# Order and buffers in a Strassen-form feed-forward layer: a product moved, a fifth weight buffer, and the first difference of a weight tile made first

## The chip, the cores and the metric

The kernel runs on one core of one Trainium2 chip. The metric is the device time of one execution in microseconds (us). Kernel before: 956.69 us, the median of three runs (956.43 to 957.4).

## The reference

One layer of a hybrid decoder over 1,024 tokens and 16 learned meta tokens, width 1,024, all in float32:

```python
u = rmsnorm(h, g_pre_mix[l])
z = u @ w_in[l]
q, k, v, xr, yr = jnp.split(z, split_at, axis=-1)
attn = sliding_window_attention_with_sinks(...)      # window 128, 8 heads of 64
hr = rg_lru(causal_depthwise_conv(xr, ...), ...)     # linear recurrence over the tokens
rec = (jax.nn.gelu(yr.astype(jnp.float32)) * hr).astype(h.dtype)
mix = jnp.concatenate([attn.astype(h.dtype), rec], axis=-1) @ w_out[l]
h = h + rmsnorm(mix, g_post_mix[l])
u = rmsnorm(h, g_pre_ffn[l])
f = jnp.square(jax.nn.relu(u @ w_ff1[l])) @ w_ff2[l]
h = h + rmsnorm(f, g_post_ffn[l])
```

The feed-forward part is 1,024 × 1,024 × 4,096 and back; its two matrix products take most of the time, and the change is there.

## The kernel before

**Numbers.** Every float32 operand of a product is taken apart into a high and a low part in the type fp32r (`split`, L96 and L99): ScalarE casts the tile (high), then VectorE subtracts the cast from the tile (low). A product is then three matmuls (`mm3`, L125 to L127): high × high, high × low, low × high. `product` makes four of these, for four chunks of 128 rows: twelve matmuls with 512 columns.

**Strassen form.** The first product `u @ w_ff1` is done by a Strassen–Winograd scheme over 2 × 2 blocks: seven products of blocks where the plain way has eight, for sums and differences of blocks of weights and of activations. The weights of w_ff1 go through in 16 pairs of chunks (p = 0 to 15), each 128 columns of the left and of the right half. For each pair the products add up into four blocks ("11", "12", "21", "22"), which are later activated (relu, square) and go into w_ff2. The second product has the same form, written as a table of seven steps for each of eight quarters (`PLAN`, `steps`): 56 steps, each with a weight tile from one or two loads. Where there are two, they are combined on VectorE, or added on the way by an accumulating DMA of GpSimd.

**First loop of w_ff1.** `prep_a(p)` makes what pair p needs. It loads two 512 KB tiles by SyncE's queue (`w1_load`, L989): r0, in a buffer named "raw" (two of these), which holds the blocks a11 and a21, and r1 ("a" or "d") with a12 and a22. Four combines (L992, VectorE, 128 × 512 each) follow: a22 + a21, a21 − a11, a3 = that sum − a11, and a12 − a3. Two splits: r0 into a pair of "ws" buffers (128 × 1024; high on ScalarE, low on VectorE), and a3 into one "e" buffer that holds its high and low part. r1, which now has the changed a12 and a22, is stored to `s_dram` by GpSimd's queue (L1037), for the second loop.

The loop over p then issues, for each pair: product with e (a3), a ScalarE copy of the accumulator to block "12" (L1177), product `p1(p+2)` of a11 (which needs ws of that pair), product with the ws columns of a21, and a copy to block "21" (L1181). So an iteration on TensorE is three products. For the first four pairs p1 and p2 ("early" products, with weights loaded ahead: `a11_early`, `a12_early`) are done before the loop. p2 adds its product to block "11" on VectorE (L1106).

Six pieces of other work, `t_rest`, are spread over the iterations p = 3 to 8: four differences of activations, and two splits whose results go to `t4_dram` for a later stage (L1168).

**What sets the order.** The framework places each engine's instructions by priority and by a model of when operands are ready; each engine then runs its list in order. `behind(name, instruction)` adds an edge of order only: the instruction stands after the named one. In w_ff2, `prep_2` puts a combine behind the low part of two steps before (L1264 is the load there, `w_lows`). SyncE and GpSimd issue their DMAs in the order of their lists, and a DMA waits at the head of its list until its buffer is free.

**Buffers.** One table has the number of buffers by name: "raw" 2, "ws" 4, "a" 16, "b" 17, "c" 8, "d" 4, "e" 3. A tile takes the buffers of its name in turn, and waits for the last reader of the tile that had that buffer.

Of the kernel before, what the change touches and what calls it, by code (L numbers as in the profile page):

```python
# [10 lines left out]
F32R = mybir.dt.float32r  # L11
AF = mybir.ActivationFunctionType
ALU = mybir.AluOpType
# [3 lines left out]
P = 128  # L17
# [20 lines left out]
def hybrid_layer(  # L38
# [6 lines left out]
    nc = tc.nc  # L45
# [6 lines left out]
    ps = ctx.enter_context(tc.tile_pool(name="ps", bufs=2, space=PSUM))  # L52
    dpool = ctx.enter_context(tc.tile_pool(name="dpool", bufs=1, space=DRAM))

    bufs = {"raw": 2, "ws": 4, "a": 16, "b": 17, "c": 8, "d": 4, "e": 3}
    uid = [0]

    def slot(tag, shape, dt=F32):
        uid[0] += 1
        return slab.tile(shape, dt, tag=tag, name=f"{tag}{uid[0]}", bufs=bufs[tag])  # L60

    def pair(tag, shape):
        return slot(tag, shape, F32R), slot(tag, shape, F32R)

    def bank(tag, shape=(P, 512)):
        uid[0] += 1
        return ps.tile(list(shape), F32, tag=tag, name=f"ps_{tag}{uid[0]}")

    def f32(ap):
        return ap.bitcast(F32)  # L70
# [23 lines left out]
    def split(hi, lo, src, eng=None):  # L94
        if eng is None:
            nc.scalar.copy(hi, src)  # L96
        else:
            eng.tensor_copy(hi, src)
        low = nc.vector.tensor_tensor(lo, src, f32(hi), op=ALU.subtract).ins  # L99
        mark[0] = low.name  # L100
        return low
# [4 lines left out]
    def behind(name, *inss):  # L106
        for ins in inss:
            tc.add_manual_dep(
                ins, name,
                mybir.DependencyInfo(  # L110
                    mybir.DependencyClass.NoSync, mybir.DependencyReason.DATA
                ),
                reason="order",
            )
# [5 lines left out]
        ).ins  # L120
        return high, low

    def mm3(dst, lhs, rhs, start, stop):
        (lh, ll), (rh, rl) = lhs, rhs
        nc.tensor.matmul(dst, lh, rh, start=start, stop=False, skip_group_check=True)  # L125
        nc.tensor.matmul(dst, lh, rl, start=False, stop=False, skip_group_check=True)  # L126
        last_mm[0] = nc.tensor.matmul(  # L127
            dst, ll, rh, start=False, stop=stop, skip_group_check=True
        ).ins.name

    last_mm = [None]
# [129 lines left out]
    def project(w, pieces, sink):  # L261
        wh, wl = w
        for t0, n in pieces:
            acc = bank("acc")
            for kc in range(KC):
                uh, ul = u[kc]
                mm3(
                    acc[:, :n], (wh[:, kc, :], wl[:, kc, :]),
                    (uh[:, t0 : t0 + n], ul[:, t0 : t0 + n]),
                    kc == 0, kc == KC - 1,  # L270
                )
            sink(acc[:, :n], t0, n)
# [70 lines left out]
    def low_w(w, raw):  # L343
        chained(1, nc.vector.tensor_tensor(w[1], raw, f32(w[0]), op=ALU.subtract).ins)
# [58 lines left out]
    low_w(wv, rv)  # L403
    wq = high_w(rq)
    low_w(wq, rq)
    km = slot("e", [P, 4, 2 * P], F32R)
    nc.gpsimd.memset(f32(km[:, 0:2, 0 : P - NMETA]), 0.0)
    nc.gpsimd.memset(f32(km[:, 2:4, :]), 0.0)
    nsink = const.tile([P, 8], F32, name="nsink")
# [84 lines left out]
    for b in range(4):  # L494
# [3 lines left out]
        if b == 0:  # L498

            acc = [bank("acc"), bank("acc")]  # L500
# [11 lines left out]
            for w, (t0, n), sink, tag in (  # L512
                (wq, (16, 256), sink_q0, "o"), (wx, piece, sink_x0, "acc"),
            ):
                acc = bank(tag)
# [397 lines left out]
    t4_dram = dpool.tile([P, 2, 4, 512], F32, name="t4_dram")  # L913
# [73 lines left out]
    def w1_load(dst, b, p, a0, a1):  # L987
        c0 = 256 * p
        nc.sync.dma_start(dst, w1v[b][:, :, c0 + P * a0 : c0 + P * a1])  # L989

    def combine(dst, x0, x1, op):
        return nc.vector.tensor_tensor(dst, x0, x1, op=op).ins  # L992

    def operand(tiles):
        pairs = []
        for t_ in tiles:
            hi, lo = pair("b", [P, 2, 512])
            split(hi, lo, t_)
            pairs.append((hi, lo))
        return pairs  # L1000

    def product(acc, w, op, first):
        wh, wl = w
        for kc in range(4):
            hh, ll = op[kc // 2]
            mm3(
                acc, (wh[:, kc, :], wl[:, kc, :]), (hh[:, kc % 2, :], ll[:, kc % 2, :]),
                first and kc == 0, kc == 3,
            )

    LO, HI = slice(0, P), slice(P, 2 * P)
# [3 lines left out]
    def prep_a(p, late=None):  # L1015
        r0 = slot("raw", [P, 4, 256])
        w1_load(r0, 0, p, 0, 2)
        r1 = slot("a" if 2 <= p < 6 else "d", [P, 4, 256])
        w1_load(r1, 1, p, 0, 2)
        a11, a21, a12, a22 = r0[:, :, LO], r0[:, :, HI], r1[:, :, LO], r1[:, :, HI]  # L1020
        sums = [
            combine(a22, a21, a22, ALU.add), combine(a21, a11, a21, ALU.subtract)
        ]
        if late:
            behind(late, *sums)
        hi, lo = pair("ws", [P, 4, 256])
        if p in a11_early:
            split(hi[:, :, HI], lo[:, :, HI], a21)
            first = a11_early[p]
        else:  # L1030
            split(hi, lo, r0)
            first = hi[:, :, LO], lo[:, :, LO]
        combine(a11, a22, a11, ALU.subtract)
        hl = slot("e", [P, 2, 4, P], F32R)
        split(hl[:, 0], hl[:, 1], a11)
        combine(a12, a12, a11, ALU.subtract)
        nc.gpsimd.dma_start(s_dram[p], r1)  # L1037
        return first, (hl[:, 0], hl[:, 1]), (hi[:, :, HI], lo[:, :, HI])


    def early(b, p0, hl):
        raw = slot("raw", [P, 2, 4, P])
        for k in range(2):
            w1_load(raw[:, k], b, p0 + k, 0, 1)
        split(*hl, raw)
        return {p0 + k: (hl[0][:, k], hl[1][:, k]) for k in range(2)}

    a11_early, a12_early = {}, {}

    def fetch_b(p):  # L1050
        r1 = slot(("e", "raw")[p % 2], [P, 4, 256])
        nc.sync.dma_start(r1, s_dram[p])
        return r1
# [24 lines left out]
    def block(k, p):  # L1078
        q = p // 2
        if fb[k][q] is None:  # L1080
            fb[k][q] = slot(FTAG[k][q], [P, 2, 512])
        return fb[k][q][:, p % 2, :]
# [15 lines left out]
    def p1(p, w):  # L1098
        ya[p] = bank(("acc", "s")[p // 2 % 2])
        product(ya[p], w, b11, True)  # L1100
        nc.scalar.copy(block("11", p), ya[p])

    def p2(p, w):
        y2 = bank("pt")
        product(y2, w, b21, True)
        nc.vector.tensor_tensor(block("11", p), y2, block("11", p), op=ALU.add)  # L1106

    for t in range(8):
# [12 lines left out]
        if t == 6:  # L1121
            b21 = operand(u2f[0][2:4])
            hl = slot("b", ESH, F32R), slot("e", ESH, F32R)
# [4 lines left out]
    for p in range(2):  # L1128
        p2(p, a12_early[p])
# [10 lines left out]

    t_sums(slice(0, 3 * P))
    wa[0] = prep_a(0)
    u2_tiles(7, xns[7])
    t_sums(slice(3 * P, 4 * P))
# [1 line left out]
    for p in range(2, 4):  # L1146
        p1(p, a11_early[p])
    a12_early.update(early(1, 2, pair("a", ESH)))
    for p in range(2, 4):
        p2(p, a12_early[p])  # L1150
    ot3 = [pair("b", [P, 2, 512]) for _ in range(2)]
    for i in range(2):
        behind(urgent, split(*ot3[i], t3[i]))
# [3 lines left out]
    def t_rest(k):  # L1157
        i = k % 2
        if k < 2:
            behind(mark[0], combine(u2f[1][i], u2f[1][i], u2f[0][i], ALU.subtract))  # L1160
        elif k < 4:
            behind(mark[0], combine(t2[i], u2f[0][2 + i], t2[i], ALU.subtract))
        else:
            hl = pair("a", [P, 2, 512])
            late = mark[0]
            behind(late, split(*hl, t2[i]))
            for n in range(2):
                nc.sync.dma_start(t4_dram[:, n, 2 * i : 2 * i + 2, :], f32(hl[n]))  # L1168

    raw_b, raw_c = {}, {}  # L1170
    for p in range(16):
        if p + 2 < 16:
            wa[p + 2] = prep_a(p + 2, None if p else urgent)
        if p >= 13:
            raw_b[p - 13] = fetch_b(p - 13)
        product(ya[p], wa[p][1], ot2, False)
        nc.scalar.copy(block("12", p), ya[p])  # L1177
        if 4 <= p + 2 < 16:
            p1(p + 2, wa[p + 2][0])
        product(ya[p], wa[p][2], ot3, False)  # L1180
        nc.scalar.copy(block("21", p), ya[p])  # L1181
        if 3 <= p < 9:
            t_rest(p - 3)

        if p == 14:
            ot1 = operand(u2f[1][0:2])
# [81 lines left out]
    def prep_2(n, tag="ws"):  # L1268
        i, q = steps[n]
        fx, wx, _ = PLAN[i]  # L1270
        raws = raw_2.pop(n)
        if len(raws) == 2:
            ins = combine(raws[0], raws[0], raws[1], wx[2])
            if i == 6:
                behind(w_low[0], ins)
            elif i > 2:
                behind(w_lows[n - 2], ins)
        wh, wl = pair(tag, [P, 2, 512])
        w_low[0] = w_lows[n] = split(wh, wl, raws[0]).name
        if len(fx) == 3:  # L1280
            f = slot("b", [P, 2, 512])
            combine(f, fb[fx[0]][q], fb[fx[1]][q], fx[2])
        else:
            f = fb[fx[0]][q]
        fh, fl = pair("b", [P, 2, 512])
        split(fh, fl, f)
        return fh, fl, wh, wl
# [11 lines left out]
    for n, p in enumerate(third):  # L1299
# [8 lines left out]
        if p not in a12_early:  # L1308
            y2 = bank(("acc", "s")[p % 2])
# [195 lines left out]
```

## Time and profile before

| | |
|---|---|
| median of three runs | 956.69 us (956.43 to 957.4) |
| the profiled execution | 955.87 us, of which 954.1 us between the first and the last instruction |
| granted clock of TensorE | 0.999 |
| TensorE busy | 944.0 us, 4728 matmuls |
| VectorE / ScalarE / GpSimd busy | 657.8 / 504.2 / 125.4 us |
| moved by DMA | 130.21 MB, mean 136 GB/s |
| first loop of w_ff1 | about 350 to 475 us |

How to read a line: a timeline row gives start, duration, engine, line of the kernel, operation, output ← inputs, shapes, and in brackets how long the engine was idle before and what it waited for. A row of waits gives who waited for whom, the sum in us, how often, and the longest. A row of stretches gives the stretch, its length, busy time and count for TensorE, its weight loads, VectorE, ScalarE and GpSimd, then the granted clock, the busy share of the DMA engines and GB/s. TensorE's matmuls overlap: one of 512 columns is listed with about 0.39 us, and starts come every 0.23 us. "Issue to landing" of a DMA is told by the trace only for some of them.

### The profile page before, as it was taken

The numbers are of one execution on the slowest core, as the hardware profiler recorded it, in microseconds if no ns is written. First come the engines' busy times: TensorE is split into PE (matmuls) and PEld (weight loads), VectorE is DVE, ScalarE is ACT, GpSimd is POOL, SyncE is SP. The second block draws the span as 40 slices with busy tenths as digits, with TensorE's granted clock in tenths as the row PEclk, the third lists the DMA queues.
The fourth block names the chain that finished last, engine by engine and source line by source line (L and its number), as shares of the span: only waits on it lengthen the run. The fifth ranks groups of instructions, "written<-read, shape, count | busy, mean of one in ns | idle before, by whom it ended". The sixth has DMA issues, their size and how long they took to land.

```text
span 954.1 us, 12400 instructions
## 1 busy us (share of the span) xinstructions
PE 944.0 (99%) x4728; PEld 789.3 (83%) x4728; DVE 657.8 (69%) x845; ACT 504.2 (53%) x854; POOL 125.4 (13%) x184
## 2 busy tenths in 40 slices
PE   9999999999999999999999999999999999999997
PEld 8999999877888877888888878888888888888885
DVE  6567987779866776665644465477567676779893
ACT  8537766478645554443555575663533343446441
POOL 4103564320020100000000000001111000001201
PEclk9999999999999999999999999999999999999999
DMA  8221011104225366675522354325677665537924
GB/s 273 56 67 24 23 45 46 45 23 140 81 110 177 133 220 199 198 257 162 208 100 89 111 180 129 111 88 151 164 190 172 192 210 178 197 134 196 244 45 89
DMA packets 88200, 130.21 MB, mean 136 GB/s; under 512 B 13703, under 2 KB 52631, under 8 KB 88141
## 3 DMA queue, kind: packets, MB, share of 16 engines
q1 hardware_dynamic: 79548, 106.54, 33.5%
q0 software_dynamic: 8160, 21.57, 10.8%
q10 hardware_dynamic: 432, 1.31, 0.4%
q8 instruction: 37, 0.61, 0.2%
q14 instruction: 23, 0.18, 0.1%
HBM read 109.93 MB, written 18.87 MB: 135 GB/s over the span
## 4 chain that ended last, share of the span: by engine, by line
PE 94%; DVE 2%; ACT 1%; POOL 1%; DMA 1%; issue 0%; DVEq 0%; SPq 0%; POOLq 0%; ACTq 0%
PE ps_acc L125 11%; PE ps_acc L126 11%; PE ps_acc L127 11%; PE ps_pt L125 7%; PE ps_pt L126 7%; PE ps_pt L127 7%; PE ps_s L125 6%; PE ps_s L127 6%; PE ps_s L126 6%; PE ps_o L127 5%; PE ps_o L125 5%; PE ps_o L126 5%; PE ps_o L687 1%; PE ps_acc L278 1%; DMA b<-t_dram 1%; POOL c L676 1%
## 5 line engine op out<-in xcount | busy, mean ns | idle before, releaser
L96 ACT CAST ws<-raw 128x1024 fp32r<-128x1024 f32 (+1 forms) x68 | 69.6, 1024 | 124.1 <-PE ps_o L126 49.4
L99 DVE TENSOR_TENSOR ws<-raw,ws 128x1024 fp32r<-128x1024 f32 (+1 forms) x69 | 82.4, 1194 | 61.7 <-ACT ws L96 60.6
L125 PE MATMUL ps_acc<-a,ws 128*128 128x256 f32 (+2 forms) x256 | 85.8, 335 | 0.0
L126 PE MATMUL ps_acc<-a,ws 128*128 128x256 f32 (+2 forms) x256 | 85.2, 333 | 0.0
L127 PE MATMUL ps_acc<-a,ws 128*128 128x256 f32 (+2 forms) x256 | 85.2, 333 | 0.0
L99 DVE TENSOR_TENSOR b<-b,b 128x1024 fp32r<-128x1024 f32 (+2 forms) x50 | 58.9, 1177 | 29.0 <-PE ps_o L126 20.1
L96 ACT CAST ws<-e 128x1024 fp32r<-128x1024 f32 x41 | 42.9, 1047 | 65.4 <-PE ps_o L126 42.1
L96 ACT CAST b<-b 128x1024 fp32r<-128x1024 f32 (+2 forms) x49 | 50.0, 1020 | 39.9 <-DVE b L992 34.4
L99 DVE TENSOR_TENSOR ws<-e,ws 128x1024 fp32r<-128x1024 f32 x41 | 50.1, 1222 | 22.1 <-ACT ws L96 22.1
L676 POOL TENSOR_SCALAR_AFFINE_SELECT c<-c 128x512 fp32r<-128x512 f32 x64 | 51.9, 831 | 70.4 <-ACT c L96 60.9
L125 PEld LDWEIGHTS ps_acc<-a,ws 128*128 128x128 f32 x256 | 48.3, 189 | 4.6 <-issue 0.2
L127 PEld LDWEIGHTS ps_acc<-a,ws 128*128 128x128 f32 x256 | 48.2, 188 | 4.5
L126 PEld LDWEIGHTS ps_acc<-a,ws 128*128 128x128 f32 x256 | 48.1, 188 | 4.5 <-issue 0.4
L125 PE MATMUL ps_acc<-ws,b 128*128 128x512 f32 (+1 forms) x120 | 46.2, 386 | 0.0
L127 PE MATMUL ps_acc<-ws,b 128*128 128x512 f32 (+1 forms) x120 | 46.2, 385 | 0.0
L126 PE MATMUL ps_acc<-ws,b 128*128 128x512 f32 (+1 forms) x120 | 46.1, 384 | 0.0
L125 PE MATMUL ps_pt<-ws,b 128*128 128x512 f32 x112 | 44.4, 396 | 0.0
L126 PE MATMUL ps_pt<-ws,b 128*128 128x512 f32 x112 | 44.1, 394 | 0.0
L127 PE MATMUL ps_pt<-ws,b 128*128 128x512 f32 x112 | 44.0, 393 | 0.0
L125 PE MATMUL ps_s<-ws,b 128*128 128x512 f32 x110 | 43.4, 395 | 0.0
L127 PE MATMUL ps_s<-ws,b 128*128 128x512 f32 x110 | 43.3, 394 | 0.0
L126 PE MATMUL ps_s<-ws,b 128*128 128x512 f32 x110 | 43.3, 393 | 0.0
(414 smaller groups left out, 2660.9 us busy)
## 6 DMA issues: line engine op xcount, KB each, us to landing
raw<-in_w_ff_dram SPq DMA_DIRECT2D x61, 512.0 KB, 4.8
e<-in_w_ff_dram SPq DMA_DIRECT2D x45, 512.0 KB, 3.5
d<-in_w_ff_dram SPq DMA_DIRECT2D x12, 512.0 KB
s_dram<-d POOLq DMA_DIRECT2D x12, 512.0 KB, 4.1
c<-in_x_dram SPq DMA_DIRECT2D x8, 512.0 KB, 3.4
raw<-in_w_in_dram SPq DMA_DIRECT2D x8, 512.0 KB
d<-in_x_dram SPq DMA_DIRECT2D x8, 512.0 KB, 3.3
out_dram<-raw SPq DMA_DIRECT2D x8, 512.0 KB
```

What stands on the lines that cost most here:

```text
L96: nc.scalar.copy(hi, src)
L99: low = nc.vector.tensor_tensor(lo, src, f32(hi), op=ALU.subtract).ins
L125: nc.tensor.matmul(dst, lh, rh, start=start, stop=False, skip_group_check=True)
L126: nc.tensor.matmul(dst, lh, rl, start=False, stop=False, skip_group_check=True)
L127: last_mm[0] = nc.tensor.matmul(dst, ll, rh, start=False, stop=stop, skip_group_check=True).ins.name
L278: last_mm[0] = nc.tensor.matmul(acc[:, :n], w[k // 2][:, kc, :], u[kc][k % 2][:, t0 : t0 + n], start=k == 0 and kc == 0, stop=k == last an ...
L676: nc.gpsimd.affine_select(out=p_[:, :, s], in_=f32(p_[:, :, 0]), pattern=[[0, 4], [g, P]], compare_op=op, fill=0.0, base=0, channel_multip ...
L687: nc.tensor.matmul(po[:, oc : oc + n], v, p_[:, pc : pc + n], start=first and k == 0, stop=last and k == 1, skip_group_check=True,)
```

## The change

1. The early product p2 of pair 3 no longer stands ahead of the loop; it is issued inside pair 0, after the copy of block "12", and its first matmul is put behind the last matmul of the product before.
2. "ws" has five buffers, "e" two. The tiles have the same size, so the memory is the same. The mask tile km of attention moves from "e" to "ws".
3. In `prep_a`, for the twelve pairs p = 4 to 15, a21 − a11 is made first; then a3 = a22 − (a21 − a11) into the place of a21, and a22 = a3 + a11 last. Four combines, as before. r1 is in an "a" buffer for p = 2 to 13 (before: 2 to 5).
4. The four stores to `t4_dram` go to GpSimd's queue.
5. In w_ff2 only the combine of step 21 is put behind the low part of two steps before; before, all combines of the steps of i = 3 to 5 were.

```diff
-    bufs = {"raw": 2, "ws": 4, "a": 16, "b": 17, "c": 8, "d": 4, "e": 3}
+    bufs = {"raw": 2, "ws": 5, "a": 16, "b": 17, "c": 8, "d": 4, "e": 2}
...
-    def mm3(dst, lhs, rhs, start, stop):
+    def mm3(dst, lhs, rhs, start, stop, after=None):
         (lh, ll), (rh, rl) = lhs, rhs
-        nc.tensor.matmul(dst, lh, rh, start=start, stop=False, skip_group_check=True)
+        ins = nc.tensor.matmul(
+            dst, lh, rh, start=start, stop=False, skip_group_check=True
+        ).ins
+        if after:
+            behind(after, ins)
...
-    km = slot("e", [P, 4, 2 * P], F32R)
+    km = slot("ws", [P, 4, 2 * P], F32R)
...
-        r1 = slot("a" if 2 <= p < 6 else "d", [P, 4, 256])
+        r1 = slot("a" if 2 <= p < 14 else "d", [P, 4, 256])
         w1_load(r1, 1, p, 0, 2)
         a11, a21, a12, a22 = r0[:, :, LO], r0[:, :, HI], r1[:, :, LO], r1[:, :, HI]
-        sums = [
-            combine(a22, a21, a22, ALU.add), combine(a21, a11, a21, ALU.subtract)
-        ]
+        near = p in a11_early
+        sums = [combine(a22, a21, a22, ALU.add)] if near else []
+        sums.append(combine(a21, a11, a21, ALU.subtract))
...
-        combine(a11, a22, a11, ALU.subtract)
+        if near:
+            a3 = a11
+            combine(a3, a22, a11, ALU.subtract)
+        else:
+
+            a3 = a21
+            combine(a3, a22, a21, ALU.subtract)
+            combine(a22, a3, a11, ALU.add)
         hl = slot("e", [P, 2, 4, P], F32R)
-        split(hl[:, 0], hl[:, 1], a11)
-        combine(a12, a12, a11, ALU.subtract)
+        split(hl[:, 0], hl[:, 1], a3)
+        combine(a12, a12, a3, ALU.subtract)
         nc.gpsimd.dma_start(s_dram[p], r1)
...
-    for p in range(2, 4):
-        p2(p, a12_early[p])
+    p2(2, a12_early[2])
...
-                nc.sync.dma_start(t4_dram[:, n, 2 * i : 2 * i + 2, :], f32(hl[n]))
+                nc.gpsimd.dma_start(t4_dram[:, n, 2 * i : 2 * i + 2, :], f32(hl[n]))
...
         nc.scalar.copy(block("12", p), ya[p])
+        if p == 0:
+            p2(3, a12_early[3], last_mm[0])
...
-            elif i > 2:
+            elif n == 21:
                 behind(w_lows[n - 2], ins)
```

`p2` passes `after` to `product`, and that to the first `mm3`. Lines of the kernel after are those of before plus 4 (L989, L992) to 12 (L1264).

More of the change, by code (lines that the diff above doesn't have):

```diff
@@ L1000, in operand, with product @@
         return pairs
-    def product(acc, w, op, first):
+    def product(acc, w, op, first, after=None):
         wh, wl = w
@@ L1007, in product @@
                 acc, (wh[:, kc, :], wl[:, kc, :]), (hh[:, kc % 2, :], ll[:, kc % 2, :]),
-                first and kc == 0, kc == 3,
+                first and kc == 0, kc == 3, after if kc == 0 else None,
             )
@@ L1101, in p1, with p2 @@
         nc.scalar.copy(block("11", p), ya[p])
-    def p2(p, w):
+    def p2(p, w, after=None):
         y2 = bank("pt")
-        product(y2, w, b21, True)
+        product(y2, w, b21, True, after)
         nc.vector.tensor_tensor(block("11", p), y2, block("11", p), op=ALU.add)
```

## The prediction

> **What bounds the kernel now.** I read the page first, then the waits of TensorE, then busy time by stretches of 25 us, then the timeline of one iteration.
>
> ```profile
> span 954.1 us, 12400 instructions
> PE 944.0 (99%) x4728; PEld 789.3 (83%) x4728; DVE 657.8 (69%) x845; ACT 504.2 (53%) x854; POOL 125.4 (13%) x184
> ```
> ```profile
> PE ps_acc L304 <- DVE base_e L558: 1.5, 1, 1.5
> PE ps_acc L125 <- ACT a L1177: 0.7, 1, 0.7
> PE ps_pt L1225 <- DMA b<-t_dram: 0.5, 1, 0.5
> PE ps_o L687 <- POOL c L676: 0.3, 1, 0.3
> ```
> ```profile
> 375.00:400.00 25.00, 25.00 (x110) 20.25 (x109) 15.79 (x21) 10.73 (x16) 1.29 (x3) 1.00 0.59 190
> 400.00:425.00 25.00, 25.00 (x109) 20.25 (x108) 16.32 (x21) 10.70 (x17) 2.03 (x4) 1.00 0.76 252
> 425.00:450.00 25.00, 25.00 (x109) 20.29 (x108) 12.29 (x17) 9.26 (x14) 1.16 (x3) 1.00 0.60 189
> ```
>
> TensorE works all the time at a granted clock of 1.00, and its number of matmuls and columns does not change here. All its listed waits sum to 3.0 us; the 1.5 at the start and the wait inside attention (L687) are outside the edited code. So the change can gain at most 0.7 + 0.5 = 1.2 us, plus little at the two ends. It can lose much more: anything that feeds TensorE late costs its full lateness. The question is therefore which feed has little to spare. I measure a gain or loss against 0.2%, 1.9 us, about what this kernel's runs can tell from no change.
>
> One iteration of the first feed-forward loop in the trace (VectorE, then SyncE's and GpSimd's issues, ScalarE, TensorE):
>
> ```profile
> 379.44 1.23 DVE L99 TENSOR_TENSOR ws<-raw,ws 128x1024 fp32r<-128x1024 f32 x1 [2.86 <-ACT ws L96]
> 380.59 0.69 DVE L992 TENSOR_TENSOR d<-raw,d 128x512 f32<-128x512 f32 x1
> 381.19 0.69 DVE L992 TENSOR_TENSOR raw<-d,raw 128x512 f32<-128x512 f32 x1
> 381.79 0.69 DVE L992 TENSOR_TENSOR raw<-raw 128x512 f32<-128x512 f32 x1
> 382.39 0.69 DVE L992 TENSOR_TENSOR d<-d,raw 128x512 f32<-128x512 f32 x1
> 383.00 0.69 DVE L99 TENSOR_TENSOR e<-raw,e 128x512 fp32r<-128x512 f32 x1
> 383.60 1.22 DVE L992 TENSOR_TENSOR c<-c,c 128x1024 f32<-128x1024 f32 x1
> 387.80 1.23 DVE L99 TENSOR_TENSOR ws<-raw,ws 128x1024 fp32r<-128x1024 f32 x1 [2.98 <-ACT ws L96]
> ```
> ```profile
> 375.48 0.37 SPq L989 DMA_DIRECT2D raw<-in_w_ff_dram  x1
> ...
> 383.71 0.37 SPq L989 DMA_DIRECT2D raw<-in_w_ff_dram  x1
> ```
> ```profile
> 383.48 0.53 POOL L1037 DMA_DIRECT2D s_dram<-d  x1 [8.26 <-DVE d L992]
> ```
> ```profile
> 378.36 1.05 ACT L96 CAST ws<-raw 128x1024 fp32r<-128x1024 f32 x1 [2.00 <-PE ps_acc L126]
> ```
> ```profile
> 381.61 0.39 PE L127 MATMUL ps_s<-b,ws 128*128 128x512 f32 x1
> ...
> 389.97 0.39 PE L127 MATMUL ps_s<-b,ws 128*128 128x512 f32 x1
> ```
>
> The reader is to see three things. TensorE takes its first low part of the cast weights at 381.61 and the next at 389.97: an iteration is 8.36 us. The low part is done at 380.67, only 0.94 us ahead. And what holds it is the buffer: ScalarE's cast begins at 378.36 when TensorE gives one back. The raw tile of the next weights is no limit here: its load was issued at 375.48 and the first subtraction on it runs at 381.79 in VectorE's third place after the low part, with 6.3 us for the load.
>
> **The change, part by part.**
>
> *The last early product inside pair 0.* The second product of pair 0 waits for ScalarE to copy block "12" (0.7 us in the waits above). Twelve matmuls of p2(3) are put there; they are moved, not added. Gain 0.7, and the block add that follows them moves behind with them, at no cost: nothing reads block "11" of pair 3 for many iterations.
>
> *Five buffers for cast weights, two for e.* A round of five gives a high part the buffer of an old low part and a low part that of an old high part. The wait of 2.00 before the cast goes and the low part can start about a microsecond earlier. In itself it gains nothing, since TensorE does not wait for it. In attention the mask tile now takes one of the five, which leaves four as before; zero.
>
> *t4_dram stores on GpSimd's queue.* Four stores leave SyncE's queue, where loads stood behind them, and stand between the s_dram stores; each issue takes about the 0.53 of the row above, on an engine busy 13%. What moves is their traffic: below.
>
> *W2's combines.* All but one ordering edge of the combines is dropped, and in the compiled order four combines now stand ahead of the low part of two steps before, each waiting for a load.
>
> ```profile
> 775.14 0.40 PE L126 MATMUL ps_acc<-ws,b 128*128 128x512 f32 x1
> ```
> ```profile
> 769.75 1.23 DVE L99 TENSOR_TENSOR ws<-e,ws 128x1024 fp32r<-128x1024 f32 x1 [1.48 <-ACT ws L96]
> ```
> ```profile
> DMA to landing us min/median/max: 3.1/3.8/7.0
> ```
> The low part now has 775.14 − 770.98 = 4.2 us to spare, and the loads of this line (the last row, of L1264) land in 3.8. By my count the four steps use up some 3.6 of the 4.2: I take zero, with 1.5 as the upper bound if a load takes about 4.5.
>
> *Twelve pairs with the first difference first.* The four combines and two splits stay; same work. What matters is the order that the compiled program gets on VectorE. For the pairs from the seventh to the eleventh and the thirteenth to the fifteenth it is, with k the pair whose weights are split and k+1 the next:
>
> ```
> raw(k+1): first difference        <- waits for the load of raw(k+1)
> ws(k): low part                   <- TensorE needs this
> raw(k): a3;  a22;  a12
> e(k): low part                    -> frees the buffer of raw(k); load of raw(k+2) is issued
> ```
> Before, the low part of ws(k) stood ahead of all work on raw(k+1); now it stands behind it. There are two raw buffers, so raw(k+1) can only be loaded when e(k−1) is done. That closes a circle: low part, three combines, e's low part, load, first difference, next low part. Its length from the rows above: three combines at their pitch of 0.60 = 1.80, e 0.69, issue 0.03 (383.69 to 383.71), the load L, one more difference 0.60, the low part 1.23: 4.35 + L. It must not exceed the 8.36 of TensorE, so L must be at most 4.01. Filling work (the 1.22 combine after e) lies inside L and costs nothing; the fifth buffer does not help, since the circle runs over raw.
>
> How long is L? The rows nearest to it are those of the same 512 KB tile (page; then the loads of raw between 375 and 450 us):
>
> ```profile
> raw<-in_w_ff_dram SPq DMA_DIRECT2D x61, 512.0 KB, 4.8
> e<-in_w_ff_dram SPq DMA_DIRECT2D x45, 512.0 KB, 3.5
> ...
> s_dram<-d POOLq DMA_DIRECT2D x12, 512.0 KB, 4.1
> ```
> ```profile
> DMA to landing us min/median/max: 4.8/5.1/5.4
> ```
> These are only loads whose end the trace can tell. From below: 3.5, the loads of e, which mostly have no store beside them. From above: 5.4. In this loop the store of s_dram is issued 0.23 us before the load (383.48, 383.71) and will be again, as a12 is still made just before e's low part; store and load share the DMA engines. I take 4.8, the page's median for raw and the smallest in this loop.
>
> The sum. First step: the load issued at 375.48 (pair before: its e is done then, before and after) lands at 380.28, difference and low part make 382.11, against 381.61: 0.50 late. Four more steps each lose 4.35 + 4.8 − 8.36 = 0.79: 3.16. At pair 12 the order puts the low part ahead again, the circle opens, and VectorE regains about 4 us of lead; that lead is limited by the buffer (the low part takes the buffer that TensorE gives back one product, 2.78, before it needs this one; less 1.23: about 1.5). Three further steps lose 3 × 0.79 − 1.5 = 0.87. Together 4.5 us. The 0.7 gained at pair 0 is not subtracted: the circle starts from VectorE and the DMA, not from TensorE, so a TensorE that is 0.7 ahead there only waits 0.7 longer. The profiled execution took 955.87 (954.1 span and 1.8 around it) and would take 960.4; the median of the runs is 0.8 above it: **961.2**.
>
> **The rivals.**
>
> *The loads are quick enough.* For L up to 4.1 nothing is late, and the 0.7 at pair 0 remains: 956.69 − 0.7 = 956.0, on the faster side, though not by 0.2%. For it: in the loop the DMA share is 0.59 to 0.76, and e's loads land in 3.5. Against it: no told load of raw in this stage. It decides at L = 4.01 to 4.3. Between 4.1 and 4.4 the loss is under 1.9: 956.7 to 958.5. Chance of the two together 0.27. The Trainium skill ("DMA: Bandwidth & Descriptors", section "Anatomy of one DMA — SWDGE (gpsimd) path") stands on this side: it fits a DMA by 2.0 us plus its bytes at 436 GB/s, as an estimate 3.2 us for this tile, by which the circle would close in 7.55 us and the sum would be this rival's 956.0. The trace does not agree so far: no load of raw told in the loop is that short.
>
> *The stores moved to GpSimd's queue starve the loads.* Two of the four t4 stores now fall directly beside an s_dram store on one queue, while the loads of pairs 10 and 11 wait. A store lands in about 4 us by the row above; two in a row could hold a load back by up to 2 us each in a circle without slack: 961.2 + 2 to 4, so 963 to 965. Against it: half of the transfer may pass beside the store. Chance 0.12, within the slower case. The Trainium skill says on the same page ("Queues, rings and completion order") that each DMA engine goes round between its queues packet by packet; a store in larger packets than the load's would then get the larger part, which speaks for this rival.
>
> *The W2 order stalls alone.* A load of 4.5 there makes up to 1.5: 956.0 + 1.5 = 957.5; chance 0.05.
>
> *Faster by over 0.2%.* It needs 1.9 us, and the waits above leave 1.2: the t_dram wait of 0.5 would have to go too, and start or tail would have to give the rest. 954.5; chance 0.05.
>
> **How the numbers follow.** The stall in the circle has 0.63 (0.12 of it with starved loads), quick or nearly quick loads 0.27, W2 alone 0.05, faster 0.05. Faster 0.05, same 0.32, slower 0.63. The likeliest gives 961.2. The range: below, the quick loads with the 0.7 and 0.3 of the t_dram wait, 955.7; above, L = 5.4: 1.10 + 4 × 1.39 + 3 × 1.39 − 1.5 = 9.3, so 966.0, which holds the starved case as well. The slower case alone: 958.6 to 966.
>
> **What would show it.** In the profile after: the wait of the product on the copy of L1177 is gone; TensorE's waits list a new row on VectorE's low part of ws (L99), several times, 0.4 to 1.5 each, between 375 and 450 us; VectorE's waits list the first difference (now L996) behind the load of raw, about as often; the stretches of 25 us there hold 104 to 107 matmuls in place of 109. If the stretches still hold 109 and VectorE waits for raw without TensorE waiting, the loads were quick. If L1178 stores lie beside the longest loads, it was starving. I would be wrong if VectorE is well ahead at the seventh pair for a reason that I do not see, or if the load in the circle lands below 4 us because it does not meet the store.

## The result, and the profile after

The changed kernel takes 971.0 us (970.8 to 971.28, four runs) against 956.71 for the kernel before: a ratio of 1.0145 with a 95% interval of 1.0131 to 1.016. The forecast was 961.2, in 955.7 to 966.0. The sign was right, and the first loop is one of the three places where time was lost; the size was not right: 14.3 us were lost, not 4.5.

The page of the profile after, then TensorE's waits, then the stretches that were shown of before:

```profile
span 969.5 us, 12457 instructions
PE 949.2 (98%) x4728; PEld 790.7 (82%) x4728; DVE 654.5 (68%) x845; ACT 506.1 (52%) x854; POOL 128.8 (13%) x188
```
```profile
PE ps_s L131 <- DVE ws L99: 4.5, 3, 2.8
PE ps_acc L130 <- DVE ws L99: 3.5, 4, 2.0
PE ps_acc L131 <- DVE ws L99: 2.0, 3, 1.1
```
```profile
375.00:400.00 25.00, 22.23 (x90) 17.63 (x89) 12.53 (x16) 7.66 (x12) 1.59 (x3) 0.93 0.55 166
400.00:425.00 25.00, 22.50 (x95) 17.31 (x94) 15.79 (x21) 11.04 (x17) 3.14 (x6) 1.00 0.67 220
425.00:450.00 25.00, 24.40 (x106) 19.50 (x105) 13.49 (x19) 9.75 (x15) 1.65 (x4) 1.00 0.57 183
```

The wait for the copy of block "12" is gone, and ten waits for a low part of ws stand in its place: six in this loop (the rows of L131), two in w_ff2 and two at the end (L130). Where there were 109 or 110 matmuls in 25 us there are 90, 95 and 106, and one stretch has a granted clock of 0.93, which the kernel before shows nowhere in this loop.

The first stall in TensorE's timeline, and VectorE's and SyncE's beside it:

```profile
380.66 0.40 PE L131 MATMUL ps_acc<-b,e 128*128 128x512 f32 x1
383.82 0.64 PE L131 MATMUL ps_s<-b,ws 128*128 128x512 f32 x1 [2.77 <-DVE ws L99]
384.26 0.63 PE L125 MATMUL ps_s<-b,ws 128*128 128x512 f32 x1
384.69 0.63 PE L130 MATMUL ps_s<-b,ws 128*128 128x512 f32 x1
```
```profile
374.61 0.69 DVE L99 TENSOR_TENSOR e<-raw,e 128x512 fp32r<-128x512 f32 x1
375.21 1.22 DVE L996 TENSOR_TENSOR c<-c,c 128x1024 f32<-128x1024 f32 x1
381.94 0.69 DVE L996 TENSOR_TENSOR raw<-raw 128x512 f32<-128x512 f32 x1 [5.52 <-DMA raw<-in_w_ff_dram]
382.55 1.22 DVE L99 TENSOR_TENSOR ws<-raw,ws 128x1024 fp32r<-128x1024 f32 x1
```
```profile
375.32 0.37 SPq L993 DMA_DIRECT2D raw<-in_w_ff_dram  x1
375.74 1.69 SPq L993 DMA_DIRECT2D a<-in_w_ff_dram  x2
386.46 0.37 SPq L993 DMA_DIRECT2D raw<-in_w_ff_dram  x1
```

This is the circle of the prediction: e's low part ends at 375.30, the load is issued at 375.32, VectorE makes one combine of c and then stands idle until its first difference at 381.94, and the low part that TensorE waits for comes only then. And the price is more than the wait: after it the matmuls start 0.43 apart, not 0.23.

To share out the loss I take each matmul's start, less the start of the one before and less the usual 0.23, and sum what is over:

| where in the profile after | us |
|---|---|
| six gaps at 381 to 457 (2.9, 0.5, 1.3, 1.3, 0.8, 0.8) | 7.5 |
| half pace after the first of them, eight matmuls | 1.6 |
| w_ff2, 765 to 788: gaps of 0.6, 2.2, 0.4, 0.2 | 3.4 |
| half pace after these, six matmuls | 1.2 |
| the end, 910 to 934: gaps of 0.2, 0.4, 1.0 | 1.6 |
| sum (added before rounding) | 15.2 |
| saved: the copy wait (0.84) and the t_dram wait (0.67) | −1.5 |

This leaves 13.7 for a difference of the spans of 15.4. Of the rest, 0.4 lies at the start: matched matmul by matmul, TensorE is that much later than in the kernel before from 9 us on, and by 0.3 to 0.8 in the other runs matched so (e1, e3, e5, e6, e8, e9, e10). Some 1 us more comes from the ten gaps without half pace: behind each, the second matmul starts 0.34 after the first, not 0.23 (402.64 and 402.98), which the table does not count.

### The profile page after: what moved, and what is told of

Its sections match the earlier page's. It is cut to its first block, busy times and chain, and to the rows that moved or that the text cites. A ratio compares the mean times of both kernels' runs of the same rounds, so it can differ in the third digit from the quotient of the medians.

```text
span 969.5 us, 12457 instructions
## 1 busy us (share of the span) xinstructions
PE 949.2 (98%) x4728; PEld 790.7 (82%) x4728; DVE 654.5 (68%) x845; ACT 506.1 (52%) x854; POOL 128.8 (13%) x188
## 4 chain that ended last, share of the span: by engine, by line
PE 73%; DVE 9%; DMA 8%; issue 4%; ACT 3%; POOL 1%; SPq 0%; DVEq 0%; POOLq 0%; ACTq 0%
PE ps_acc L130 8%; PE ps_acc L131 8%; PE ps_acc L125 8%; DMA raw<-in_w_ff_dram 6%; PE ps_pt L130 5%; PE ps_pt L131 5%; PE ps_pt L125 5%; PE ps_o L130 5%; PE ps_o L125 5%; PE ps_o L131 5%; PE ps_s L131 4%; PE ps_s L130 4%; PE ps_s L125 4%; DVE ws L99 2%; DVE a L996 2%
## 5 line engine op out<-in xcount | busy, mean ns | idle before, releaser
L130 PE MATMUL ps_acc<-a,ws 128*128 128x256 f32 (+2 forms) x256 | 85.4, 333 | 0.0
L131 PE MATMUL ps_acc<-a,ws 128*128 128x256 f32 (+2 forms) x256 | 85.1, 333 | 0.0
L99 DVE TENSOR_TENSOR b<-b,b 128x1024 fp32r<-128x1024 f32 (+2 forms) x50 | 58.9, 1177 | 15.8 <-ACT b L96 15.2
L131 PEld LDWEIGHTS ps_acc<-a,ws 128*128 128x128 f32 x256 | 48.2, 188 | 4.5
L130 PEld LDWEIGHTS ps_acc<-a,ws 128*128 128x128 f32 x256 | 48.2, 188 | 4.4 <-issue 0.4
L130 PE MATMUL ps_acc<-ws,b 128*128 128x512 f32 (+1 forms) x120 | 47.2, 393 | 3.6 <-DVE ws L99 3.5
L125 PE MATMUL ps_acc<-ws,b 128*128 128x512 f32 (+1 forms) x120 | 46.7, 389 | 0.0
L131 PE MATMUL ps_acc<-ws,b 128*128 128x512 f32 (+1 forms) x120 | 46.6, 388 | 0.0
L131 PE MATMUL ps_pt<-ws,b 128*128 128x512 f32 x112 | 44.1, 394 | 0.0
L130 PE MATMUL ps_pt<-ws,b 128*128 128x512 f32 x112 | 44.1, 394 | 0.0
L130 PE MATMUL ps_s<-ws,b 128*128 128x512 f32 x110 | 43.5, 395 | 0.0
L131 PE MATMUL ps_s<-ws,b 128*128 128x512 f32 x110 | 43.4, 395 | 0.0
```

The lines of the kernel that those rows point to most:

```text
L125: ins = nc.tensor.matmul(dst, lh, rh, start=start, stop=False, skip_group_check=True).ins
L131: last_mm[0] = nc.tensor.matmul(dst, ll, rh, start=False, stop=stop, skip_group_check=True).ins.name
```

## The experiments

Ratios are to the kernel before, run side by side with each version; its medians there were 957.1 to 957.9.

**e1: the low part first.** The kernel after, plus an edge of order per pair:

```diff
+        if not near and p - 1 in ws_low:
+            behind(ws_low[p - 1], *sums)
...
-            split(hi, lo, r0)
+            ws_low[p] = split(hi, lo, r0).name
```


> The kernel after, with one edge of order added per pair: the first difference of the next raw tile stands behind the low part of the current ws. Theory (the circle on VectorE over the two raw buffers): the profile after has gaps of 2.9, 0.45, 1.3, 1.3, 0.8 and 0.8 us on TensorE between 380 and 457 us, 7.4 together, and 1.6 more from the eight matmuls at half pace after the first; all of it goes and the time is 971.0 - 9 = 962. Rival (the loads themselves are late, because of the stores on GpSimd's queue or the two e buffers): the gaps stay, moved to other instructions; 969 to 971.

963.8 us, ratio 1.0061 (1.0038 to 1.0083). VectorE's waits between 375 and 460 us, first of the kernel after, then of this one:

```profile
DVE raw L996 <- DMA raw<-in_w_ff_dram: 35.5, 8, 5.5
DVE ws L99 <- PE ps_acc L130: 1.9, 1, 1.9
```
```profile
DVE ws L99 <- PE ps_acc L130: 14.4, 6, 3.9
DVE ws L99 <- PE ps_s L130: 10.7, 4, 4.4
DVE raw L996 <- DMA raw<-in_w_ff_dram: 6.9, 6, 2.5
```

Same loads, same stores, same buffers, another order: VectorE again waits for TensorE to give a buffer back, and not for the loads. In the first loop two gaps of 0.4 are left. The order makes the stalls of the loop. The time is 1.8 above the 962 expected; the gaps at the end are larger here, 2.7 together where the kernel after has 1.6.

**e2: the edges of w_ff2 restored.** In the kernel after:

```diff
-            elif n == 21:
+            elif i > 2:
```


> The kernel after, with the ordering edges of the combines in w_ff2 restored (all of i = 3 to 5). Theory: the gaps at 765 to 788 us (0.6, 2.2, 0.4, 0.2 and 1.5 of half pace, 4.9 together) come from combines that stand ahead of a low part; they go, and the time is 971.0 - 4.9 = 966.1. Rival (the accumulating loads of GpSimd come late because e has two buffers): the gap at the first of them stays and perhaps half of the others; 968 to 971.

966.9 us, ratio 1.0097 (1.0073 to 1.0121). No wait of TensorE is listed between 560 and 900. TensorE's waits:

```profile
PE ps_s L131 <- DVE ws L99: 5.1, 3, 2.7
PE ps_acc L131 <- DVE ws L99: 2.8, 3, 1.7
PE ps_acc L308 <- DVE base_e L562: 1.5, 1, 1.5
PE ps_acc L130 <- DVE ws L99: 1.4, 2, 1.2
```

The first two rows are the first loop, which lost somewhat more here (gaps of 8.8 in place of 7.5); the last one is the end.

**e3: both edits.**

> The kernel after with both edits. If the two are independent: 971.0 - 9 - 4.9 = 957.1, that is 0.4 above the kernel before: the gaps at the end (1.6) remain and the copy wait (0.7) is gained. If a stall early only hides one later (a slower stage gives the loads time), less is regained: 959 to 962.

958.4 us, ratio 1.001 (0.9998 to 1.0021). The two losses are independent and add up: as ratios, e1 regains 0.0084, e2 0.0048, and both together 0.0135. What remains over the kernel before is the end: gaps of 0.5, 0.4 and 0.5.

**e4: the order of the first difference alone**, put into the kernel before (with r1 in the "a" buffers; the t4_dram stores on SyncE, four ws and three e buffers).

> The kernel before with the order of the first difference alone (and r1 in the a buffers), without the other parts. Its compiled order has the same circle on VectorE, one pair longer. Theory: it alone makes the stalls of the first loop, 956.7 + 7 to 10 = 964 to 967. Rival (it needs the stores on GpSimd's queue or the e buffers to get late): 956 to 959.

967.7 us, ratio 1.0098 (1.007 to 1.0127), 0.7 above the expected range, and VectorE's waits for the loads in the loop are nearly those of the kernel after:

```profile
DVE raw L992 <- DMA raw<-in_w_ff_dram: 36.0, 9, 5.0
```

Nine gaps of 0.4 to 2.2 sum to 10.0, with no half pace behind any. So the circle needs neither the moved stores nor the buffers; at the pairs where the moved stores should have starved the loads the gaps are larger here, 1.5 and 2.2, than in the kernel after with them, 1.3 and 1.3.

**e5: the buffers alone**, in the kernel before.

```diff
-    bufs = {"raw": 2, "ws": 4, "a": 16, "b": 17, "c": 8, "d": 4, "e": 3}
+    bufs = {"raw": 2, "ws": 5, "a": 16, "b": 17, "c": 8, "d": 4, "e": 2}
...
-    km = slot("e", [P, 4, 2 * P], F32R)
+    km = slot("ws", [P, 4, 2 * P], F32R)
```


> The kernel before with five ws and two e buffers (mask tile in ws) and nothing else. Its compiled order has no circle in the first loop, but the end of GpSimd's queue is changed: all four accumulating stores of out stand ahead of the five accumulating loads of the last weights. Theory: the first loop runs without a gap, the low part gets more than the 0.94 us of lead, and that gains nothing; the late accumulating loads cost 1.0 to 2.7 at 895 to 930 us as in the runs before: 957.7 to 959.4. Rival (the buffers are harmless, the gaps at the end are a late effect of other parts): 956.7.

960.2 us, ratio 1.0032 (1.0019 to 1.0044), 0.8 over the expected. The gaps at the end are there (0.3, 0.4, 1.0), so they belong to the buffers. Two more, of 0.6 at 350 and 1.1 at 435 us, were not foreseen: with these buffers the framework chooses another order in the first loop as well.

**e6: the early product alone**, in the kernel before.

> The kernel before with only the early product of pair 3 moved into pair 0. Theory: the wait for the copy of block 12 goes, 0.7 to 0.84 us: 956.0. Rival (VectorE, busy back to back there, becomes the next to be late): under 0.3 gained.

960.2 us, ratio 1.003 (1.0015 to 1.0044): slower, where the theory and the rival both expected a gain. The gap of 0.84 that ended at 347 is gone, but the compiled order changed far behind the edit. At pair 9 the kernel before has e's low part ahead of the next pair's combines; here it stands behind them (kernel before, then this one):

```profile
407.15 0.69 DVE L99 TENSOR_TENSOR e<-raw,e 128x512 fp32r<-128x512 f32 x1
...
408.89 0.68 DVE L992 TENSOR_TENSOR d<-raw,d 128x512 f32<-128x512 f32 x1
```
```profile
405.91 0.69 DVE L996 TENSOR_TENSOR raw<-d,raw 128x512 f32<-128x512 f32 x1
409.97 0.69 DVE L996 TENSOR_TENSOR d<-raw,d 128x512 f32<-128x512 f32 x1 [3.38 <-DMA d<-in_w_ff_dram]
410.58 0.69 DVE L996 TENSOR_TENSOR d<-d,raw 128x512 f32<-128x512 f32 x1
411.19 0.68 DVE L996 TENSOR_TENSOR raw<-raw 128x512 f32<-128x512 f32 x1
411.79 0.68 DVE L99 TENSOR_TENSOR e<-raw,e 128x512 fp32r<-128x512 f32 x1
```

VectorE stands 3.38 us before a load (d) with TensorE's operand behind it. In the loop four gaps of 0.4 to 1.5, 3.0 together, follow. That these come from the order alone was not tested by itself.

**e7: the edges of w_ff2 alone taken off**, in the kernel before.

> The kernel before with only the ordering edges of w_ff2 taken off but for step 21. Its order on VectorE has the combine of step n+2 ahead of the low part of n from step 24 to 54, for longer than in the kernel after. Theory 1 (the order alone makes the gaps): 4 us or more, 961 or above, with gaps of 1 to 2 us from 765 on. Theory 2 (the order only hurts where the accumulating loads came late before, as they do with two e buffers: the last one landed at 748 before and at 764 after): the 4.2 us of lead bear it, 956.7 to 958.

959.0 us, ratio 1.0022 (1.0011 to 1.0033). Three gaps of 0.5, 0.9 and 0.4 at 820 to 844, none at 765: between the two theories. The order alone costs 1.75. In the kernel after, a like order meets accumulating loads of GpSimd that come later, the last one issued at 758.13 in place of 742.93, with TensorE only some 8 us behind by then:

```profile
742.93 1.21 POOL L1261 DMA_DIRECT2D raw<-in_w_ff_dram  x1 [6.36 <-DMA raw<-in_w_ff_dram]
```
```profile
758.13 1.22 POOL L1273 DMA_DIRECT2D raw<-in_w_ff_dram  x1 [7.18 <-DVE b L996]
```
```profile
764.00 1.05 ACT L96 CAST ws<-raw 128x1024 fp32r<-128x1024 f32 x1 [10.40 <-DMA raw<-in_w_ff_dram]
```

(Kernel before; kernel after, GpSimd and ScalarE.) The buffers alone (e5) make no gap there either; together with the order the loss is 4.5. That the later loads make the difference is inferred: no run has these two parts together and nothing else. e1, without the circle, still has two gaps of 1.6 and 1.7 at this place.

**e8: a longer circle.** The kernel after, with its order held by edges (not in the cut below), and from pair 6 on one more instruction that reads the raw tile:

```diff
...
         split(hl[:, 0], hl[:, 1], a3)
+        if p >= 6:
+            nc.vector.tensor_tensor(hl[:, 1], a3, f32(hl[:, 0]), op=ALU.subtract)
```


> The kernel after, with e's low part made twice (the same subtraction again) from pair 6 on, and the order of the first differences held as it was. The second subtraction reads the raw tile, so the buffer is freed later: by its pitch of 0.61 us, and in four steps by 1.16 more, since the 1.22 us combine that stood in the shadow of the load now stands ahead of it. Theory (the circle sets the pace): four steps of +1.77, one of +1.2 and two of +0.6 = 9.5, so 971.0 + 9.5 = 980.5. Rival (VectorE has room, 68% busy; the loads are late for another reason): 971 to 973.

977.6 us, ratio 1.0208 (1.019 to 1.0226), 6.6 more than the kernel after. The direction and the kind are those of the circle: VectorE, busy 68%, had no room for 0.6 us per pair. The size is not that of the theory. The first gap is 1.3 where the kernel after has 2.9 (its load took 5.2, not 6.6, to the first use); the other gaps of the loop grew from 4.5 to 10.3, against 9.5 more expected, and with the half pace the loop lost about 4 more in all. The rest is in w_ff2 and at the end.

**e9: GpSimd's queue at the end.** e3's kernel, with accumulating stores of out put behind the accumulating loads of weights (`pool_acc` holds the names of these loads, in order):

```diff
...
-        nc.gpsimd.dma_start(out[t * P : (t + 1) * P, :], o, accum_op=ALU.add)
+        ins = nc.gpsimd.dma_start(out[t * P : (t + 1) * P, :], o, accum_op=ALU.add).ins
+        if j > 1:
+            behind(pool_acc[-1], ins)
```


> The kernel with both orders mended (low parts first in the first loop, the edges of w_ff2 restored), and GpSimd's queue at the end in another order: the accumulating stores of out for the third and fourth tile stand behind accumulating loads. Theory: the gaps of 0.5, 0.4 and 0.5 at 896 to 920 us go, 1.4 less than the 958.4 of the kernel with both orders mended: about 957. Rival (the loads come late for lack of free buffers): no change, 958.4.

956.4 us, ratio 0.9991 (0.9982 to 1.0001). No gap after 400 us. The first accumulating load of the last weights in e3's kernel, and here:

```profile
886.91 1.21 POOL L1277 DMA_DIRECT2D b<-in_w_ff_dram  x1 [8.38 <-issue]
```
```profile
881.41 1.23 POOL L1280 DMA_DIRECT2D b<-in_w_ff_dram  x1 [11.14 <-DMA b<-in_w_ff_dram]
```

So the end was the order of GpSimd's queue: with two e buffers the four stores got ahead of the five loads, which are issued 6 to 9 us apart, one after the other.

**e10: four ws and three e buffers, both orders mended.** e3's kernel with the old table of buffers: the early product, the order of differences and the moved stores are kept.

> The kernel with both orders mended, with four ws and three e buffers again. Its GpSimd queue at the end is that of the kernel before. Theory: the gaps at the end go and the copy wait is gained, so 0.7 under before, 956.0. Rival (the fifth ws buffer gave the first loop the lead that it needs in the new order): gaps appear between 380 and 460, 958 or more.

956.3 us, ratio 0.998 (0.997 to 0.999): by the ratios 0.2% faster than the kernel before and 1.6% faster than the kernel after. The rival's 958 is out. What the 0.2% would come from, the profiles do not show: the span is 954.8 against 954.1 before, the copy wait of 0.8 that ended at 347 is gone, but another wait for a copy, of 0.8, ends at 409, and the t_dram wait of 0.7 is left. The medians of the kernel before itself lie 1.2 apart, 956.7 to 957.9. So the loss is undone; a gain over the kernel before is not shown.

**e11: a stall made by hand**, in the kernel before: the low part of one pair of the second loop five times.

> The kernel before, with the low part of one pair of the second loop (about 505 us) made five times (the same subtraction again): late by 4 x 1.22 - 0.94 = 3.9 us. Theory (the half pace of TensorE in the kernel after follows an idle time over some 2 us): a gap of 3.9 and then about eight matmuls at 0.43 in place of 0.23 us, 1.6 more: 956.7 + 5.5 = 962.2, with a granted clock under 1.00 in that stretch. Rival (the half pace came from the loads, not from the idle time): 960.6.

961.1 us (one run). It did not come as one gap but as several (TensorE's timeline, then two stretches):

```profile
500.55 0.50 PE L125 MATMUL ps_o<-b,ws 128*128 128x512 f32 x1 [0.32 <-DVE c L1200]
...
504.50 0.50 PE L125 MATMUL ps_o<-b,ws 128*128 128x512 f32 x1 [0.90 <-ACT ws L96]
...
505.93 0.50 PE L127 MATMUL ps_pt<-b,ws 128*128 128x512 f32 x1 [0.71 <-DVE ws L1060]
...
507.05 0.63 PE L127 MATMUL ps_pt<-b,ws 128*128 128x512 f32 x1
507.48 0.63 PE L125 MATMUL ps_pt<-b,ws 128*128 128x512 f32 x1
```
```profile
500.00:505.00 5.00, 3.78 (x15) 2.47 (x14) 4.93 (x6) 3.39 (x4) 0.00 (x0) 1.00 0.01 3
505.00:510.00 5.00, 4.29 (x12) 3.21 (x12) 2.02 (x2) 1.90 (x2) 0.00 (x0) 0.66 0.55 170
```

The gaps sum to 2.4 and the seven matmuls at half pace add 1.4, with a granted clock of 0.66 in that stretch. The waits are for VectorE and ScalarE, and the DMA engines were all but idle (share 0.01) while they fell. So the half pace comes from TensorE's idle time and not from the loads. The time alone, 961.1, lies between the theory and the rival and would not decide it.

## Why the prediction was wrong

*What bounds the kernel, and where it could lose.* Right: TensorE bound, little to gain (1.5 was saved, counted from start to start, where 1.2 of listed waits was the limit), and the low part of ws as the feed with least to spare in the first loop.

*The early product.* Its 0.84 was gained. "At no cost" did not hold by itself (e6): the edit moves the compiled order far away from it. In the whole change no such cost is seen apart from the others.

*The buffers.* "In itself it gains nothing": right. Priced at zero for losses too, and that failed: the end of GpSimd's queue (1.6 in the kernel after; e5 and e9) was not in the sum at all, though the order was there to be read.

*The stores on GpSimd's queue.* Rightly left out of the sum; the rival of starved loads falls with e4. The two loads with those stores beside them took 5.2 to their first use in the kernel after, and 5.5 and 6.1 in e4, where the stores are on SyncE's queue.

*The first difference.* The mechanism was right: e1 takes the circle away by order alone, e4 makes it alone, e8 makes it longer. The term was 4.5 and came to 7.5. L was taken as 4.8, the shortest of the told loads of raw in this loop (4.8 to 5.4); the words "no told load of raw in this stage" hold only for loads under 4.1. In the first step VectorE's first difference came 6.6 after the issue, and that one gap is 2.9 where 0.5 was forecast: 2.4 of the 3.0. In the others it came 4.7 to 5.2 after the issue, and VectorE's own part of the circle was 4.5 (381.94 to 386.46), not 4.35. The next four steps came to 3.0 against 3.2, in part by luck: one had no gap, after TensorE had been slowed, and two had 1.3 each, not 0.79. The last two gaps make 1.5 against 0.9. A packet of the instruction queue, 16 KB and 0.93 us long, falls into the first load in the kernel after and in e2 (both 6.6), and at its very end in e4 (5.2). That it delays one of the DMA engines is possible and was not tested; the load issued at 415.02 in the kernel after met such a packet too and took 5.2.

*W2's combines.* This is the step that failed most plainly: "I take zero, with 1.5 as the upper bound". It came to 4.5, and e2, which restores the edges, regains 4.1. e7 loses 1.75 to the order with the old buffers, at 820 to 844, so the order by itself already passes the upper bound. I had counted the lead as it was in the kernel before, 4.2, and took for granted that the buffers leave the accumulating loads in time. They came later in the kernel after; that this took the lead away is the likely rest, not shown by a run of its own. The parts were priced one by one and the bounds did not add their meeting.

*The half pace.* Not in the prediction: 1.6 + 1.2 = 2.8.

Sum of what was missing: 3.0 in the circle, 4.5 with half pace in w_ff2, 1.6 at the end, 1.6 half pace in the loop, 10.7; less the 1.5 saved that the forecast did not subtract, 9.2. The profiled execution, 971.28, is 10.9 over the 960.4 forecast for it; the 1.7 between is what the table of the profile leaves as the rest.

## What to carry to other kernels

Where one engine's list is in order, read the compiled list for every instruction that waits for a load and stands ahead of something the bound engine needs, and close the circle: if the load's issue depends on work behind that instruction, its whole time from issue to landing is in the period. A change of buffers or of one product moves such lists and queues far from the edit, so price the order that was compiled, all engines to the end of the kernel, and not the edit. Here edges of order in two places and the old buffers undo a loss of 1.5% (e10).

## What the runs showed of the hardware that I had not expected

TensorE goes on at half pace after it has been idle for a short time: matmuls of 512 columns start 0.43 us apart, not 0.23, for some 3 us. It was seen after one wait of 2.77 and after one of 1.99 (kernel after), after 2.71 (e2), after 2.37 and after 1.95 (e8), and after three of 0.3 to 0.9 within 5 us (e11). It was not seen after waits of 2.02 (e4, ending at 423.49) and 2.58 (e8, ending at 424.03). Each time it cost 1.2 to 1.6 us more. The Trainium skill ("TensorE: Matmul & The Clock Gate", section "What's actually happening") has a clock gate that halves the clock after an idle window of about 3.4 us. The half pace agrees, 0.43 against 0.23; a whole window of idle time was not needed: waits of 1.6 to 2.8 us in it were enough here.

The traces also show why a wait of 1.99 did it and one of 2.58 did not. The granted clock is 0.50 for stretches of 3.41 us, and where one run has two of them, their starts are a whole number of 3.413 us apart: 384.03 and 779.98 in the kernel after (116 times), 453.07 and 790.99 in e8 (99 times). In e2 the clock drops at 385.01, when TensorE had been back at full pace for 1.1 us. Stretches on this grid, first of the kernel after, then of e2, of e4 (counted back from the drop of its clock behind the last matmul, at 962.13) and of e8 (counted back from 453.07):

```profile
380.62:384.03 3.41, 0.64 (x3) 0.21 (x3) 2.05 (x3) 1.04 (x1) 0.00 (x0) 1.00 0.70 240
384.03:387.44 3.41, 3.41 (x9) 2.64 (x9) 3.38 (x5) 1.10 (x2) 0.53 (x1) 0.50 0.05 18
```
```profile
385.01:388.42 3.41, 3.41 (x10) 2.63 (x9) 2.64 (x4) 1.36 (x3) 0.53 (x1) 0.50 0.26 86
```
```profile
419.41:422.82 3.41, 2.06 (x9) 1.32 (x7) 1.21 (x2) 1.71 (x3) 0.00 (x0) 1.00 0.97 356
422.82:426.24 3.42, 2.75 (x12) 2.27 (x13) 3.35 (x6) 0.74 (x2) 0.35 (x1) 1.00 0.90 274
```
```profile
422.35:425.77 3.42, 1.74 (x8) 1.43 (x8) 3.35 (x5) 2.15 (x3) 0.00 (x0) 1.00 1.05 365
```

The edge at 422.82 cuts e4's wait into 1.35 and 0.67, and of e8's 2.58 only 1.68 fall into one stretch, whereas each half-pace stretch follows one with waits of 1.61 (e11) to 2.77 (kernel after). So what counts in these runs is the idle time within one such stretch, about half of it. Where a wait falls on the grid differs from run to run: the waits that end at 383.82 (kernel after) and 383.91 (e2) are followed by edges at 384.03 and 385.01. The exact limit stays open: e11's 1.61 was enough, e8's 1.68 was not.

A load of raw with a store issued 0.2 us ahead of it, by another engine, took 4.7 to 5.2 us to its first use in the circle of the kernel after, but for the first with 6.6; in e2 it took 4.9 to 5.8 and once 6.6, in e4 4.7 to 6.1. Nothing as short as the 3.5 of the loads of e was met there.
